# Gathered tokens, gate table and buffers of a PEER layer on Trainium2: 92 instead of 88 tokens gathered, from half of the heads on

## The chip, the cores and the metric

One core of one Trainium2 chip (trn2). The time is that of one execution of the whole program on the device, in microseconds (us). A tile here is 128 x 2048 float32, 1.05 MB.

## The reference

Two blocks on 256 tokens of width 2048, all in float32. Block 1 mixes a short gated convolution with block-sparse attention; block 2 mixes a Conformer convolution with an S5 state-space branch and then adds a PEER layer; a last RMSNorm gives the output. The change lies in the PEER layer: each of 8 heads picks, for each token, 16 of 128 x 128 experts by a product of two key sets, and the experts' rows are combined.

```
q = (xb @ w_q).reshape(PEER_TOKEN_BLOCK, PEER_HEADS, 2, PEER_HALF)
s = jnp.einsum('thcd,hcnd->thcn', q, sub_keys).astype(jnp.float32)
s_top, i_top = lax.top_k(s, PEER_TOPK)
cand = s_top[:, :, 0, :, None] + s_top[:, :, 1, None, :]
...
best, pos = lax.top_k(cand, PEER_TOPK)
expert = jnp.take_along_axis(cand_idx, pos, axis=-1)
gates = jax.nn.softmax(best, axis=-1).astype(xb.dtype)
act = jax.nn.gelu(jnp.einsum('td,thkd->thk', xb, u_tab[expert]))
return jnp.einsum('thk,thkd->td', gates * act, v_tab[expert])
```

## The kernel before

SP streams all weights in an order written out in `order`, one tile a `step()`. The first 192 steps (dense layers, ending with the PEER query projection `peer_q`) split each tile into two parts on ScalarE and VectorE (L189, L195); TensorE then multiplies by `mm_wide` (L293, L294: 512 and 256 columns) or `mm_perm` (L278 to L280: three of 256). Then comes PEER, which treats two sets of tokens in two ways.

**Dense tokens** (168): all 16384 experts are computed. 128 u-steps (L1577) give u.h for 128 experts each, ScalarE applies gelu (L1580), `weigh` (L1391, L1395, VectorE) multiplies by the gate table, and 128 v-steps (L1594) sum into six PSUM banks. The gate table, experts x tokens, is made by `gbuild`: for four tokens at a time, one-hots of their picks (L1348, L1358 on VectorE; L1355 and L1356 on ScalarE), four matmuls that give 128 x 128 tables (L1375), and an evacuation (L1376). Sixteen tokens make a block; eight blocks go to DRAM (`gd`, L1379) and come back per 16 u's (`gload`, L1385); the blocks of the last 40 tokens (`STAY`) remain on chip.

**Gathered tokens** (88, `NS_`): POOL gathers the picked rows of u and v by indirect DMAs (L1416), 128 rows an item, 176 items; for u VectorE takes the dot with the token's h, replicated into `x_rep` (`rows`, L1423; item at L1449), for v it adds the scaled rows (L1461, L1463). Groups of 32, 32, 16 and 8 tokens differ in how many partitions a token has. Five slots take gathers in turn. `hand_out` writes the lists of rows to gather once all eight heads of the first 128 tokens are picked (`topk`, `picks`). At the end `join_rows` adds the partitions of groups 2 and 3 by TensorE (L1516, L1521); those of groups 0 and 1 go to DRAM (`sd`) and back as four quarters (L1488, L1493); then the norm (L1498, L1499) and the output.

The order: 58 u-steps (`NU0`) with top-k and `gbuild` woven in; 70 pairs of one v and one u; 56 v alone; the last two v's go bank by bank in `join` and `turn`, where each bank's sum has the residual (`xq`, loaded at L1628 to L1631) added (L1666), is transposed (L1673) and normed. The class `Weave` interleaves: `gbuild` yields a cost per iteration, and a u-step gives it a budget of 4200; the sparse generator is *paced*: each step credits 0.78 x 2350, an item costs 2350. Each engine runs its instructions in program order, and POOL issues its DMAs in program order. A reference line of a matmul is two instructions on TensorE.

Of the kernel before, what the change touches and what calls it, by code (L numbers as in the profile page):

```python
# [18 lines left out]
P = 128  # L19
# [7 lines left out]
GROUPS = [(0, 32), (32, 32), (64, 16), (80, 8)]  # L27
NS_ = 88
# [16 lines left out]
class Weave:  # L45
# [78 lines left out]
def body(ctx, tc, xT, par, wst, kst, bblk, cblk, gfin, uexp, vexp, out):  # L124
# [104 lines left out]
    free_units = [S[24][:, k * T:(k + 1) * T] for k in range(NRING, 8)]  # L229
# [15 lines left out]
    def step(mm, evac, budget=2600.0, fine=0.0):  # L245
# [8 lines left out]
        ws["n"] += 1  # L254
        pend.append(evac)
# [875 lines left out]
    xrow = drp.tile([NS_, D], F32, name="xrow")  # L1131
    sd = drp.tile([4, 64, D], F32, name="sd")
# [95 lines left out]
    LCOL = [0, 64, 128, 160]  # L1228
    def hand_out(c):


        V = nc.vector
        if c == 0:
            V.scalar_tensor_tensor(out=flat(ab[:, 0]), in0=flat(idx[:, 0]), scalar=float(P), in1=flat(idx[:, 1]),
                                   op0=ALU.mult, op1=ALU.add)
            V.tensor_copy(flat(abu[:, 0]), flat(ab[:, 0]))
        else:
            V.tensor_copy(abr[:, P:2 * P], flat(gat))
        for g in range(2):
            hand_to(c, g)  # L1240
            if c == 0 and g == 0:
                sp_start()
        for g in range(2, len(GROUPS)):
            hand_to(c, g)

    def hand_to(c, g):
# [519 lines left out]
```

## Time and profile before

| | us |
|---|---|
| median of 3 runs (lowest, highest) | 2525.20 (2523.16, 2533.76) |
| profiled execution, its own time | 2530.83 |
| its span on the core | 2528.9 |
| TensorE busy | 2445.0 (97%) |
| VectorE busy | 1586.5 (63%) |
| ScalarE busy | 700.2 (28%) |
| mean granted TensorE clock | 0.991 |

The span is what the profiler saw; the other durations lie within it. Busy time is an average over very different stages; the windows further below tell them apart. A wait is idle time of an engine in front of an instruction, put down to what ended it.

### The profile page before, as it was taken

The numbers are of one execution on the slowest core, as the hardware profiler recorded it, in microseconds if no ns is written. First come the engines' busy times: TensorE is split into PE (matmuls) and PEld (weight loads), VectorE is DVE, ScalarE is ACT, GpSimd is POOL, SyncE is SP. The second block draws the span as 40 slices with busy tenths as digits, with TensorE's granted clock in tenths as the row PEclk, the third lists the DMA queues.
The fourth block names the chain that finished last, engine by engine and source line by source line (L and its number), as shares of the span: only waits on it lengthen the run. The fifth ranks groups of instructions, "written<-read, shape, count | busy, mean of one in ns | idle before, by whom it ended". The sixth has DMA issues, their size and how long they took to land.

```text
span 2528.9 us, 40512 instructions
## 1 busy us (share of the span) xinstructions
PE 2445.0 (97%) x16864; PEld 2322.2 (92%) x16864; DVE 1586.5 (63%) x2764; ACT 700.2 (28%) x1047; POOL 657.0 (26%) x856
## 2 busy tenths in 40 slices
PE   8999999999999999999998999999999999999997
PEld 7888878899999999988998999999999999999887
DVE  6857777589999987657768874534453434324423
ACT  5544455443334445454201640000000000000002
POOL 1788888310000000140122121212122312022000
PEclk9999999999999999999999999999999999999998
DMA  6455555565555444555599999999999999999983
GB/s 237 168 199 184 183 183 210 193 238 210 199 206 179 183 168 181 185 202 193 215 336 418 370 380 417 421 382 421 418 421 415 396 386 414 365 344 398 387 259 125
DMA packets 108187, 719.91 MB, mean 285 GB/s; under 512 B 13308, under 2 KB 14572, under 8 KB 24668
## 3 DMA queue, kind: packets, MB, share of 16 engines
q1 hardware_dynamic: 65764, 474.57, 49.9%
q0 software_dynamic: 34288, 220.73, 22.3%
q10 hardware_dynamic: 7952, 22.02, 2.4%
q8 instruction: 133, 2.18, 0.3%
q14 instruction: 50, 0.41, 0.0%
HBM read 687.10 MB, written 25.91 MB: 282 GB/s over the span
## 4 chain that ended last, share of the span: by engine, by line
PE 71%; DMA 19%; DVE 7%; issue 2%; ACT 1%; POOL 1%; SPq 0%; DVEq 0%; POOLq 0%; ACTq 0%
PE b L1577 14%; PE b L293 13%; PE b L1594 12%; DMA s<-in_vexp_dram 7%; PE b L294 7%; DMA s<-in_wst_dram 6%; PE b L278 4%; PE b L280 4%; PE b L279 4%; DVE s L195 2%; PE b L271 2%; PE b L423 2%; PE b L270 2%; PE b L269 2%; DMA s<-s 2%
## 5 line engine op out<-in xcount | busy, mean ns | idle before, releaser
L1577 PE MATMUL b<-s,s 128*128 128x168 f32 x4096 | 609.2, 308 | 14.0 <-DMA s<-in_wst_dram 13.6
L1594 PE MATMUL b<-s,s 128*128 128x168 f32 x4096 | 605.1, 307 | 17.3 <-DMA s<-in_vexp_dram 15.9
L1594 PEld LDWEIGHTS b<-s,s 128*128 128x128 f32 x4096 | 588.3, 190 | 30.4 <-issue 27.0
L1577 PEld LDWEIGHTS b<-s,s 128*128 128x128 f32 x4096 | 590.6, 191 | 21.4 <-issue 20.4
L293 PE MATMUL b<-s,s 128*128 128x512 f32 x1680 | 599.7, 400 | 0.0
L294 PE MATMUL b<-s,s 128*128 128x256 f32 x1680 | 472.0, 281 | 9.6 <-DVE s L195 9.6
L195 DVE TENSOR_TENSOR s<-s,s 128x2048 fp32r<-128x2048 f32 x192 | 453.3, 2363 | 27.2 <-issue 12.5
L293 PEld LDWEIGHTS b<-s,s 128*128 128x128 f32 x1680 | 316.1, 188 | 72.8
L189 ACT ACTIVATE s<-s 128x2048 fp32r<-128x2048 f32 x192 | 365.7, 1905 | 9.6 <-DMA s<-in_wst_dram 9.1
L1449 DVE CUSTOM_DVE_ANT_0 s<-s,s 128x2048 f32<-128x2048 f32 x88 | 201.1, 2290 | 261.0 <-DMA s<-in_uexp_dram,rbuf 209.9
L294 PEld LDWEIGHTS b<-s,s 128*128 128x128 f32 x1680 | 317.7, 189 | 13.8 <-DVE s L195 13.0
L1463 DVE SCALAR_TENSOR_TENSOR s<-s,sqsum,s 128x2048 f32<-128x2048 f32 x84 | 197.4, 2350 | 120.8 <-DMA s<-in_vexp_dram,rbuf 120.3
L1580 ACT ACTIVATE s<-b 128x168 f32<-128x168 f32 x128 | 39.1, 307 | 803.7 <-PE b L1577 803.7
L278 PE MATMUL b<-s,s 128*128 128x256 f32 x896 | 256.6, 286 | 0.0
L280 PE MATMUL b<-s,s 128*128 128x256 f32 x896 | 253.5, 283 | 0.0
L279 PE MATMUL b<-s,s 128*128 128x256 f32 x896 | 253.5, 283 | 0.0
L1416 POOL DMA_INDIRECT s<-in_uexp_dram,rbuf x88 | 110.5, 1256 | 394.6 <-DVE s L1463 218.0
L1416 POOL DMA_INDIRECT s<-in_vexp_dram,rbuf x88 | 103.1, 1171 | 316.5 <-DVE sqsum L1449 224.6
L278 PEld LDWEIGHTS b<-s,s 128*128 128x128 f32 x896 | 171.8, 192 | 3.7 <-issue 2.9
L279 PEld LDWEIGHTS b<-s,s 128*128 128x128 f32 x896 | 171.9, 192 | 0.3
L280 PEld LDWEIGHTS b<-s,s 128*128 128x128 f32 x896 | 171.9, 192 | 0.0
L837 POOL TENSOR_TENSOR sqsum<-sqsum,s 128x256 f32<-128x256 f32 x28 | 59.4, 2120 | 389.7 <-ACT s L835 389.7
(310 smaller groups left out, 2511.8 us busy)
## 6 DMA issues: line engine op xcount, KB each, us to landing
s<-in_wst_dram SPq DMA_DIRECT2D x320, 1024.0 KB, 5.0
s<-in_vexp_dram SPq DMA_DIRECT2D x128, 1024.0 KB, 17.4
tabd<-s POOLq DMA_DIRECT2D x32, 256.0 KB, 4.5
s<-tabd ACTq DMA_DIRECT2D x32, 256.0 KB, 3.5
gd<-s ACTq DMA_DIRECT2D x8, 1024.0 KB, 9.9
s<-gd POOLq DMA_DIRECT2D x7, 1024.0 KB, 27.0
xd<-s POOLq DMA_DIRECT2D x4, 1024.0 KB, 9.8
s<-in_bblk_dram ACTq DMA_DIRECT2D x8, 512.0 KB, 3.6
```

The lines of the kernel that those rows point to most:

```text
L189: nc.scalar.activation(hi_of(i), raw_of(i), AF.Copy)
L195: nc.vector.tensor_tensor(out=lo_of(i), in0=raw_of(i), in1=FV(hi_of(i)), op=ALU.subtract)
L278: nc.tensor.matmul(ps, a, xh, start=(j == 0), stop=False)
L279: nc.tensor.matmul(ps, a, xl, start=False, stop=False)
L280: nc.tensor.matmul(ps, b, xh, start=False, stop=(j == len(perm) - 1))
L293: nc.tensor.matmul(ps, a, x2, start=(j == 0), stop=False)
L294: nc.tensor.matmul(ps[:, :T], b, x2[:, :T], start=False, stop=(j == len(perm) - 1))
L1416: nc.gpsimd.indirect_dma_start(out=gb[m % len(gb)][:], out_offset=None, in_=uexp if kind == "u" else vexp, in_offset=bass.IndirectOffsetOn ...
L1449: V.tensor_tensor_reduce(out=buf, in0=buf, in1=x_rep, scale=1.0, scalar=0.0, op0=ALU.mult, op1=ALU.add, accum_out=dots_[:, k:k + 1])
L1463: V.scalar_tensor_tensor(out=acc_s, in0=buf, scalar=a, in1=acc_s, op0=ALU.mult, op1=ALU.add)
L1577: nc.tensor.matmul(ps, raw[:, k * P:(k + 1) * P], nv(k)[:, NS_:T], start=(k == 0), stop=(k == KT - 1))
L1594: nc.tensor.matmul(acc[d], raw[:, d * P:(d + 1) * P], act_at(i), start=False, stop=(i == P - 1 and (d % 3 == 2 or d == KT - 1)))
```

## The change

- **Tokens**: a fifth group of 4 tokens; `NS_` 92, 184 items, 164 dense tokens. Its h rows go to 32 x 4 partitions by 32 DMAs. At a group's boundary the last v items come before the first u items of the next group, but for the last group. All h rows now come from a copy in DRAM (`hrow`).
- **Gathers**: they may start after four heads (`number`, `told`); the item loop waits in program order for what isn't told yet. Buffers come from a free list: four at first, two more after the scores, four again during `gbuild`, five after. Weight slots have a free list, too. Pace 0.74.
- **Gate table**: six blocks through DRAM, laid out so that a load serves 8 u's in one run; 68 tokens stay on chip in five pieces. Two one-hots of four on ScalarE; yield 1350 for 1650.
- **`peer_q`**: tiles 2 to 15 by `mm_perm`.
- **End**: `xrow` is loaded into another slot once 84 v's are issued, the sums of group 2 are joined later, the quarters are added at 800 a piece.

The order of u- and v-steps is the same as before. Renamed slots are left out below.

```diff
-GROUPS = [(0, 32), (32, 32), (64, 16), (80, 8)]
-NS_ = 88
+GROUPS = [(0, 32), (32, 32), (64, 16), (80, 8), (88, 4)]
+NS_ = 92
...
-        self.pace, self.paced_credit = 0.78 * 2350, 0
+        self.pace, self.paced_credit = 0.74 * 2350, 0
...
-    NSP = 8
-    STAY = [16, 16, 8]
+    NSP = 6
+    STAY = [16, 16, 16, 16, 4]
...
-    gd = drp.tile([NSP, P, P, 16], F32, name="gd")
+    gd = drp.tile([16, P, NSP, 8, 16], F32, name="gd")
...
+        nc.gpsimd.dma_start(hrow, S[18][0:NS_, :])
+        rows(0)
...
+    def number(h):
+        hs = slice(h, h + 4)
+        nc.vector.scalar_tensor_tensor(out=ab[:, 0, hs], in0=idx[:, 0, hs], scalar=float(P), in1=idx[:, 1, hs],
+                                       op0=ALU.mult, op1=ALU.add)
+        nc.vector.tensor_copy(by_part(ids, hs), parts4(ab[:, 0, hs]))
...
-                if h == 5:
+                if h == 4:
                     yield from picks(tt, 0)
+                    if tt == 0:
+                        number(0)
+                        hand_to(0, 0, 0, 16)
+                        told.add("first")
             yield from picks(tt, 4)
             if tt == 0:
-                hand_out(0)
+                number(4)
+                hand_to(0, 0, 16, 32)
+                for g in range(1, len(GROUPS)):
+                    hand_to(0, g)
+                told.add("all")
...
     def gbuild():
+        retired.update([13, 18])
+        free_b[:] = [b for b in free_b if b not in retired]
...
-                if q < 1:
+                if q < 2:
                     nc.scalar.activation(o, iota, AF.Abs, scale=-1.0, bias=i1T[:, tq])
                     nc.scalar.activation(o, o, AF.Relu, scale=ngT[:, tq], bias=gT[:, tq])
...
-            yield 1650
+            yield 1350
...
-        if i % 16 == 15 and i // 16 + 2 < 8:
-            gload(i // 16 + 2, nc.gpsimd)
+        if i % 8 == 7 and i // 8 + 2 < 16:
+            gload(i // 8 + 2, nc.gpsimd)
...
-        for kind, m in (("u", j), ("v", j - 1)):
+        pair = [("u", j), ("v", j - 1)]
+        if 0 < j < len(batches) - 1 and batches[j][0] != batches[j - 1][0]:
+            pair.reverse()
+        for kind, m in pair:
...
+    def gathers():
+        while free_b and n_gathered[0] < len(items):
+            kind, g, k = items[n_gathered[0]]
+            if "all" not in told and not ("first" in told and g == 0 and k < 16):
+                return
+            b = free_b.pop(0)
+            nc.gpsimd.indirect_dma_start(
...
             nc.gpsimd.dma_start(x_rep[n * q:n * q + n, :], S[18][t0:t0 + n, :])
+            nc.gpsimd.dma_start(x_rep[n * q:n * q + n, :], hrow[t0:t0 + n, :])
...
-        gb.extend(slots([5, 6, 7, 12, 13]))
+        free_b.extend([6, 5, 7, 18])
...
+            while n_gathered[0] <= m or (kind == "v" and "gates" not in told):
+                gathers()
+                yield None
...
-                    sums.append((m + 3, g))
+                    sums.append((m + (6 if g == 2 else 3), g, acc_s))
...
+                while n_v[0] <= 7 * TPS:
+                    yield None
...
-            yield 2350
+            yield 800
...
-        ps = mmbank2(1)
-        step(lambda wh, wl: mm_wide(ps, wh, wl, pv2, allk), ev_pq(ps, j), TOP)
+        ps = mmbank()
+        step(lambda wh, wl: mm_perm(ps, wh, wl, pv, allk), ev_pq(ps, j), TOP)
+    sp_start()
```

How the order of instructions moves, at three places. In these listings `s_...` are slots, `b_...` PSUM banks.

ScalarE in `gbuild`, between two u-steps' gelus; before (L1376 evacuates, L1355 and L1356 make a one-hot, L1580 is the gelu):

```order
L1376 ACTIVATE s_10081<-b_71 128x4x128
L1355 ACTIVATE s_10080<-iota,s_86 128x128
L1356 ACTIVATE s_10080<-s_10080,s_86 128x128
L1580 ACTIVATE s_10973<-b_66 128x168
L1376 ACTIVATE s_10081<-b_72 128x4x128
L1355 ACTIVATE s_10080<-iota,s_86 128x128
L1356 ACTIVATE s_10080<-s_10080,s_86 128x128
L1376 ACTIVATE s_10081<-b_71 128x4x128
```

The same now (L1406, L1385 and L1386, L1642):

```order
L1406 ACTIVATE s_10074<-b_72 128x4x128
L1385 ACTIVATE s_10081<-iota,s_87 128x128
L1386 ACTIVATE s_10081<-s_10081,s_87 128x128
L1385 ACTIVATE s_10081<-iota,s_87 128x128
L1386 ACTIVATE s_10081<-s_10081,s_87 128x128
L1642 ACTIVATE s_11208<-b_65 128x164
L1406 ACTIVATE s_10074<-b_71 128x4x128
```

Two one-hots, each of two operations, stand between two evacuations where one stood.

POOL, the h rows of the last group in front of its gathers; before, sixteen DMAs of 8 rows for group 3 (L1423; L1416 gathers, L1385 loads the gate table):

```order
L1416 DMA s_11192<-in_vexp_dram,rbuf 128x2048
L1416 DMA s_11193<-in_uexp_dram,rbuf 128x2048
L1423 DMA s_10077<-s_10076 8x2048 x16
L1385 DMA s_10073<-gd 128x8x256
L1416 DMA s_11194<-in_uexp_dram,rbuf 128x2048
L1416 DMA s_11195<-in_uexp_dram,rbuf 128x2048
L1416 DMA s_11196<-in_uexp_dram,rbuf 128x2048
```

Now, thirty-two of 4 rows for group 4 (L1464; L1455 gathers, L1415 loads the gate table):

```order
L1455 DMA s_11197<-in_vexp_dram,rbuf 128x2048
L1455 DMA s_11198<-in_uexp_dram,rbuf 128x2048
L1464 DMA s_10078<-hrow 4x2048 x32
L1455 DMA s_11196<-in_uexp_dram,rbuf 128x2048
L1455 DMA s_13153<-in_uexp_dram,rbuf 128x2048
L1415 DMA s_10074<-gd 128x768
L1455 DMA s_11360<-in_uexp_dram,rbuf 128x2048
L1455 DMA s_11197<-in_vexp_dram,rbuf 128x2048
```

Three of the four u gathers of the last group and all eight v gathers behind them (of which two are shown) wait on POOL behind the copies.

VectorE at the end of the sparse tokens; before, the last add of a join (L1521), then the quarters (L1493) with weighs (L1391, L1395) of later v's between and behind them:

```order
L1521 TENSOR_TENSOR s_16426<-s_16426,b_65 24x512
L1521 TENSOR_TENSOR s_16426<-s_16426,b_66 24x512
L1493 TENSOR_TENSOR s_16426<-s_16426,s_11192 64x2048
L1391 TENSOR_TENSOR s_10971<-s_10971,s_12891 128x128
L1395 TENSOR_TENSOR s_10971<-s_10971,s_11862 128x16
L1395 TENSOR_TENSOR s_10971<-s_10971,s_10081 128x16
L1395 TENSOR_TENSOR s_10971<-s_10971,s_86 128x8
L1391 TENSOR_TENSOR s_10971<-s_10971,s_12891 128x128
```

Now (L1512 the last item, L1579 the join of group 4, L1550 the quarters, L1556 the norm's product):

```order
L1512 SCALAR_TENSOR_TENSOR s_17696<-s_11196,sqsum,s_17696 128x2048
L1579 TENSOR_TENSOR s_16844<-s_16844,b_65 28x512
L1579 TENSOR_TENSOR s_16844<-s_16844,b_66 28x512
L1579 TENSOR_TENSOR s_16844<-s_16844,b_65 28x512
L1579 TENSOR_TENSOR s_16844<-s_16844,b_66 28x512
L1550 TENSOR_TENSOR s_16844<-s_16844,s_11197 64x2048
L1550 TENSOR_TENSOR s_16844<-s_16844,s_11196 64x2048
L1550 TENSOR_TENSOR s_16844<-s_16844,s_11198 64x2048
L1550 TENSOR_TENSOR s_16844<-s_16844,s_11360 64x2048
L1556 TENSOR_TENSOR s_16844<-s_16844,s_17455 92x2048
```

All weighs stand in front of this piece, as do the first joins' adds; only the norm stands between it and the closing's first add (now L1729). On TensorE the joins' matmuls stand behind the 126th v-step.

## Rows read from the trace of the kernel before

**Rows 1.** Windows by stage: start, length, busy per engine (instructions), PEclk, DMA share, GB/s.

```profile
1229.00:1545.60 316.60, 308.11 (x2215) 307.16 (x2214) 235.15 (x600) 99.88 (x207) 67.10 (x71) 0.98 0.91 352
1400.00:1470.00 70.00, 70.00 (x539) 70.00 (x538) 55.72 (x117) 48.25 (x90) 9.28 (x8) 1.00 0.98 373
1545.60:2220.10 674.50, 653.94 (x4480) 640.69 (x4480) 287.12 (x474) 22.72 (x83) 153.45 (x136) 1.00 1.00 403
2220.10:2499.10 279.00, 268.60 (x1811) 259.86 (x1810) 97.47 (x253) 6.62 (x10) 39.78 (x51) 0.99 0.92 330
...
2499.10:2528.90 29.80, 14.12 (x98) 12.22 (x96) 12.87 (x34) 9.12 (x28) 0.00 (x0) 0.78 0.13 47
```

**Rows 2.** TensorE's waits, 1545 to 2529 us: total us, times, longest.

```profile
PE b L1594 <- DMA s<-in_vexp_dram: 15.9, 34, 2.4
PE b L1577 <- DMA s<-in_wst_dram: 13.6, 28, 3.9
```

**Rows 3.** VectorE's waits, 1545 to 2529 us, same columns.

```profile
DVE s L1449 <- DMA s<-in_uexp_dram,rbuf: 196.6, 56, 44.6
...
DVE s L1463 <- DMA s<-in_vexp_dram,rbuf: 110.3, 45, 12.3
```

**Rows 4.** Timeline of TensorE, gate table and v stage: start, us, line, shapes, count.

```profile
1405.29 2.45 PE L1577 MATMUL b<-s,s 128*128 128x168 f32 x16
1407.57 1.05 PE L1375 MATMUL b<-s 128*128 128x128 f32 x8
1408.46 1.31 PE L1577 MATMUL b<-s,s 128*128 128x168 f32 x8
...
2299.56 4.83 PE L1594 MATMUL b<-s,s 128*128 128x168 f32 x32 [0.20 <-DVE s L1395]
2304.54 7.66 PE L1594 MATMUL b<-s,s 128*128 128x168 f32 x49 [0.15 <-DVE s L1395]
```

**Rows 5.** Timeline of ScalarE in the gate table: evacuation, then a one-hot.

```profile
1441.04 1.06 ACT L1376 ACTIVATE s<-b 128x512 f32<-128x512 f32 x1 [0.98 <-PE b L1375]
1441.89 0.37 ACT L1355 ACTIVATE s<-iota,s 128x128 f32<-128x128 f32 x1
1442.30 0.49 ACT L1356 ACTIVATE s<-s,s 128x128 f32<-128x128 f32 x1
```

**Rows 6.** Timeline of TensorE, triples at 799 us, pairs at 1047 us.

```profile
799.08 0.28 PE L278 MATMUL b<-s,s 128*128 128x256 f32 x1
...
802.67 0.28 PE L278 MATMUL b<-s,s 128*128 128x256 f32 x1
...
1047.68 0.40 PE L293 MATMUL b<-s,s 128*128 128x512 f32 x1
...
1053.68 0.40 PE L293 MATMUL b<-s,s 128*128 128x512 f32 x1
```

**Rows 7.** Timeline of POOL: first list, loads of xq, rows of group 3.

```profile
1252.60 2.02 POOL L1254 DMA_DIRECT2D rbuf<-s  x4 [114.70 <-DVE s L1310]
...
2218.30 0.94 POOL L1628 DMA_DIRECT2D s<-xd  x1 [45.73 <-PE b L1577]
...
2263.08 0.52 POOL L1423 DMA_DIRECT2D s<-s  x1 [6.25 <-DMA s<-in_uexp_dram,rbuf]
...
2271.27 0.52 POOL L1423 DMA_DIRECT2D s<-s  x1 [1.17 <-DMA s<-s]
```

**Rows 8.** Timeline of VectorE, group 3's first item and the end.

```profile
2284.68 2.29 DVE L1449 CUSTOM_DVE_ANT_0 s<-s,s 128x2048 f32<-128x2048 f32 x1 [25.30 <-DMA s<-s]
...
2451.11 0.69 DVE L1521 TENSOR_TENSOR s<-s,b 24x512 f32<-24x512 f32 x1 [44.47 <-PE b L1516]
...
2452.89 0.33 DVE L1395 TENSOR_TENSOR s<-s,s 128x16 f32<-128x16 f32 x3
...
2458.96 2.28 DVE L1493 TENSOR_TENSOR s<-s,s 64x2048 f32<-64x2048 f32 x1
...
2500.99 0.68 DVE L1666 TENSOR_TENSOR s<-b,s 128x504 f32<-128x504 f32 x1 [24.39 <-PE b L1594]
```

More of the change, by code (lines that the diff above doesn't have):

```diff
@@ L228, in body @@
     NRING = 4
-    free_units = [S[24][:, k * T:(k + 1) * T] for k in range(NRING, 8)]
+    free_units = [S[25][:, k * T:(k + 1) * T] for k in range(4)]
     free_pairs = []
@@ L254, in step @@
         ws["n"] += 1
+        if i in whole:
+            w_release(i)
         pend.append(evac)
@@ L1227, in body, with hand_to @@
     flat = lambda ap: ap.rearrange("p h k -> p (h k)")
[L1228 to L1246, printed above, removed]
+    LCOL = [0, 64, 128, 160, 176]
+    ids = mask.bitcast(U32)
+    by_part = lambda ap, hs: ap.rearrange("p (q h j) -> p h q j", q=4, h=8)[:, hs]
+    parts4 = lambda ap: ap.rearrange("p h (q j) -> p h q j", q=4)
+    def number(h):
[3 more added lines that the diff above has]
+        nc.vector.tensor_copy(by_part(ids, hs), parts4(ab[:, 0, hs]))
+    def hand_to(c, g, k0=0, k1=None):
         t0, n = GROUPS[g]
@@ L1316, in topk @@
             if tt == 0:
-                hand_out(1)
+                V.tensor_copy(by_part(abr[:, P:2 * P], slice(0, 8)), parts4(gat))
+                for g in range(len(GROUPS)):
+                    hand_to(1, g)
+                told.add("gates")
             yield None
@@ L1347, in gbuild @@
             t = NS_ + t4 * 4
+            if t4 == 4 * (NSP + 2):
+                while retired & set(flying):
+                    next(sp_gen)
+                kept[2:4] = slots([18, 13])
             nc.vector.tensor_tensor(
@@ L1422, in rows @@
         for q in range(P // n):
-            nc.gpsimd.dma_start(x_rep[n * q:n * q + n, :], S[18][t0:t0 + n, :])
+            nc.gpsimd.dma_start(x_rep[n * q:n * q + n, :], hrow[t0:t0 + n, :])
     def sp_start():
-        assert ws["n"] >= WU and len(q_ready) == KT and s_ready[0] == NH
-        gb.extend(slots([5, 6, 7, 12, 13]))
-        for m in range(len(gb)):
-            gather(m)
-            if m == 0:
-                rows(0)
+        assert ws["n"] == WU
+        slots([6, 5, 7, 18, 3, 4])
+        free_b.extend([6, 5, 7, 18])
+        w_free.extend([3, 4])
+        gathers()
         weave.paced.append(sp_gen)
@@ L1435, in sparse @@
         V = nc.vector
+        more = [12, 13]
         for _ in range(AHEAD):
+            gathers()
             yield None
@@ L1466, in sparse @@
                 nc.scalar.activation(dst, src, AF.Gelu_apprx_tanh)
-            if m + len(gb) < len(items):
-                gather(m + len(gb))
+            if b not in retired:
+                free_b.append(b)
+            if more and s_ready[0] == NH:
+                slots(more)
+                free_b.extend(more)
+                more = []
+            gathers()
             if kind == "u" and k == n - 1 and g < len(GROUPS) - 1:
@@ L1481, in sparse @@
                 yield 2350
-                yield from join_rows(sums.pop(0)[1], acc_s)
+                yield from join_rows(*sums.pop(0)[1:])
             yield 2350
         y = y_rows[0]
+        gb = [S[b] for b in (5, 6, 7, 12)]
         quarters = [gb[q][0:64, :] for q in range(4)]
@@ L1490, in sparse @@
             yield None
-        yield from join_rows(sums.pop(0)[1], acc_s)
+        yield from join_rows(*sums.pop(0)[1:])
         for q in range(4):
             V.tensor_tensor(out=y[0:64, :], in0=y[0:64, :], in1=quarters[q], op=ALU.add)
-            yield 2350
+            yield 800
         while not gf_there[0]:
@@ L1511, in join_rows @@
         t0, n = GROUPS[g]
-        assert u_done[0]
-        s_ = sel[:, 96 * (g - 2):96 * (g - 2) + NS_]
+        while not u_done[0]:
+            yield None
+        s_ = sel[:, NS_ * (g - 2):NS_ * (g - 1)]
         for h in range(2):
@@ L1651, in body @@
     ws["n"] += LAST
-    zs = slots([15, 16])
-    rows_o = slots([17, 8])
+    zs = slots([9, 23])
+    rows_o = slots([10, 17])
     junk = slots([12])[0]
```

123 lines of the change are left out of this document (70 added, 53 removed).

## The prediction

> **What bounds the kernel now.** I first read the windows by stage, then TensorE's waits, VectorE's waits, and last the timelines of the stages that the change touches. The stages [rows 1] are: 58 u-steps with top-k and gate table (316.6 us), 70 pairs of v and u (674.5), 56 v-steps alone (279.0), and the closing (29.8). TensorE is busy for 308.11 of 316.6, 653.94 of 674.5 and 268.60 of 279.0 us, at a granted clock of 0.98 to 1.00, its level of 2.4 GHz: its own work is the first bound. In the pairs the DMA engines are the second, with a share of 1.00 and 403 GB/s. TensorE's waits there and after are small: 15.9 and 13.6 us for weight tiles [rows 2]. VectorE in the same time waits 196.6 and 110.3 us for gathered rows [rows 3]. So both the SP queue (weights) and the POOL queue (gathers) are always filled, and a tile of 1.05 MB costs 2.60 us of DMA time (1.0486 MB / 403 GB/s). When TensorE does wait for weights, it steps at 4.98 us (2299.56 to 2304.54) instead of its own 4.56, twice the 2.28 us of 16 instructions [rows 4].
>
> **Fewer columns.** A u- or v-step is 32 instructions of 168 columns, now 164. 16 instructions of 168 columns take 2.28 us and 8 of 128 columns 0.89 us [rows 4], 142.5 and 111.2 ns each, so 0.78 ns per column; 32 x 4 x 0.78 = 0.10 us a step, and 4.46 in place of 4.56. Over 256 steps that is 25.6 us, wherever TensorE is the bound.
>
> **Query projection** (`mm_wide` to `mm_perm`). A pair of instructions takes 0.353 us (17 in 6.00 us), a triple 0.359 (10 in 3.59) [rows 6]. For 16 triples in each of 14 tiles that is +1.3 us; I take +1. The ACT copy and the VectorE add that it drops lie beside TensorE and cost nothing now.
>
> **U stage with the gate table.** By the first pair of order fences ScalarE now makes two of four one-hots: four short operations and one evacuation per four tokens instead of two and one. From start to start an evacuation takes 0.85 us, the next operation 0.41, the last at most 0.49 [rows 5]. So an iteration costs 0.85 + 2 x (0.81 to 0.90) = 2.47 to 2.65 us, plus one gelu of the u-step per 3.1 iterations (0.1 us): 2.56 to 2.74. TensorE needs 0.89 + 4.46/3.11 = 2.32 us per iteration, because the smaller yield packs 3.11 iterations into a u-step where 2.55 were (counted in the order). So ScalarE, at 48.25 of 70 us busy before [rows 1], becomes the bound of this stretch. I take the middle, 2.65: 41 x 2.65 = 109 us for the stretch, and (58 - 41/3.11) x 4.46 = 200 us for the other u-steps. Before: 42 x (0.89 + 4.56/2.55) = 113 and (58 - 42/2.55) x 4.56 = 189. Together 309 against 302: **+7**. The ends: -7 (295) if ScalarE keeps up, +10 (312) at 2.74. VectorE loses a one-hot per iteration, which hid beside TensorE. Earlier gathers (first at 1252.60 before [rows 7], after the last of the eight heads) use idle DMA time, but the order has 40 items on VectorE ahead of the first weigh (37 before) and 143 of 184 ahead of the 72nd, where the u's end (145 of 176): the slower pace of 0.74 gives the lead back.
>
> **Pairs.** By TensorE 140 x 0.10 = -14 us. By DMA 103 items instead of 108 between those two places, 5 x 2.60 = -13. Both bounds fall alike, so I take **-13**; the other end is 0, if each saved column is waited out on weights that still come at 4.98.
>
> **V stage and closing.** Here two paths run. The sparse path now: at 2220 VectorE had 31 items left, now 41. It ended with time to spare: 44.47 us of waiting for TensorE before a join, and 24.39 before the closing's first operation at 2500.99 [rows 8]. Without the first of these the closing could have begun 281 - 44 - 24 = about 212 us after 2220. Added are 10 gathers at 5.0 us, the queue's turn while both queues are full (50 us), one more join (4.3, estimated: four adds of 0.69 us [rows 8] and the matmuls that the second pair of them waits for), and the h rows of the fifth group: 32 small DMAs on POOL, in front of the gathers (second pair of fences). Group 3's sixteen are the nearest rows. Once they run, POOL issues one per 1.02 us (nine from 2263.08 to 2271.27 [rows 7]) and VectorE idled 25.30 us for them [rows 8], 1.58 each. So 33 to 51 us, with 32 x 0.52 = 17 as the floor if only the issue counts. I take 42, because the copies are half as large but as many waits stand between them. What is queued behind: gathers 173 and on, and on VectorE the weighs of the last v-steps, for which TensorE then waits too. Against it: the loads of `xq`, for which POOL waited 45.73 us on TensorE's last u-step [rows 7], block less when the sparse path is late; I take 15 of a possible 31. So 212 + 50 + 4 + 42 - 15 = 293.
> The Trainium skill, "DMA: Bandwidth & Descriptors", section "Anatomy of one DMA — SWDGE (gpsimd) path", gives a DMA issued from GpSimd about 2.0 us plus its bytes at 436 GB/s, so 32 in a row would take 66 us and the sum would be 24 us higher; the issues at 1.02 us show that several overlap here, so I do not take it.
> TensorE's path: 54 x 4.46 = 241 us and 5 to 21 of waits. But two joins and the token sums now stand behind the 126th v-step (third pair): 4.3 for a join, 2.3 for the last item, 4.3 again, 4 x 2.28 for the sums [rows 8] and some 5.5 for the norm (two operations of that length and 1 us) make 25.5 us before the closing's first add. Before, this lay in the 24 and 44 us of slack, at no cost. So 272 to 288. The later of the two paths counts: 293 against 281, and the closing behind it is the same: **+12**, with ends -9 (272, all gathers in time) and +36 (51 us of copies and no relief from `xq`, 317).
>
> **Cost nothing:** the gate blocks now come in 16 loads of 0.39 MB for 7 of 1 MB, with fewer bytes; two more weigh operations a step (three took 0.33 us [rows 8], so 0.22) on a VectorE that waits for gathers; `hrow` to DRAM, 0.75 MB beside the projection. If their cover, VectorE's 300 us of waiting, were gone, the weighs would cost 128 x 0.22 = 28 us.
>
> **Sum:** 1 + 7 - 13 + 12 = +7 on the profiled execution's 2530.8, so 2537.8. That execution lies 5.6 above the median of 2525.2; I give the median, **2532 us**.
>
> **Rivals.**
> *Faster* (0.31): ScalarE does not bind and the sparse path is done in time. For: VectorE's 44 us of slack [rows 8], and the short activations [rows 5] may follow each other faster than they did with idle time between. Against: ScalarE's sum above 2.32, and the joins behind the last steps. With the middle of 272 to 288 for the end, 1 - 7 - 14 - 1 = -21: 2504 us.
> *Slower* (0.27): the 32 row copies. Three gathers of u and eight of v stand behind them, and the last weighs, and TensorE behind those. For: 25.30 us of idle for sixteen. Against: they leave the DMA engines to the weights, so TensorE gains a lead. At 51 us with no relief: 1 + 7 - 13 + 36 = +31: 2556. It decides from about 45 us on, where the sparse path passes 300 us.
> *It doesn't do what it says* (0.06): during the gate table only four gather buffers are in turn. If the gathers are bound by their flight, four instead of five give a quarter longer per item: about 22 items x 1.1 us = 24 us, 2557. For: VectorE's waits for gathers [rows 3]. Against: in the U stage VectorE was busy 235.15 of 316.6 [rows 1] and the pace sets items.
> *My forecast*, no change that can be told: 0.36.
>
> **Range and chances.** A measurement of this kernel tells about 0.5% from no change, 12.6 us. The range of 2502 to 2560 takes in the middle of the faster case and the whole of the slower ones but the worst sums of ends; about a tenth is left out on each side. The forecast alone, with its ends for ScalarE (-14 and +3) and for the xq loads (-16 and +15), would give 2516 to 2547. Faster 0.31; same 0.36; slower 0.33, the two slow cases together.
>
> **What would show it.** Right: u-steps of 4.46 us; in the gate-table stretch TensorE waits for ScalarE's one-hots, and an iteration takes 2.5 to 2.7 us; pairs 13 us shorter; VectorE idle for the last row copies 30 to 50 us; the closing's first add 25 us or more behind the 126th v-step. Wrong: iterations of 2.32 us with no wait on ScalarE; row copies inside 20 us; the closing right behind the last v-step; or pairs as long as before, with waits for weights that ate the columns.

## The result, and the profile after

The changed kernel takes 2544.0 us (median of 7 runs, 2539.26 to 2556.5) against 2525.4 before (7 runs): a ratio of 1.0076, 95% interval 1.0054 to 1.0097. It is 19 us slower. Its profiled span is 2541.0 us against 2528.9, so 12 of the 19 us are in the traces compared here.

The stages in the profile after, in windows cut at the same places as [rows 1] (first u-step, first v-step, last u-step, end of the 126th v-step, end); the second row is a piece of the gate table's stretch. Columns are as there.

```profile
1230.40:1550.20 319.80, 306.52 (x2206) 301.33 (x2205) 223.83 (x542) 126.06 (x287) 68.80 (x73) 0.99 0.90 345
1400.00:1470.00 70.00, 65.91 (x485) 62.63 (x484) 45.94 (x92) 66.15 (x145) 5.76 (x5) 1.00 0.84 278
1550.20:2209.10 658.90, 635.31 (x4482) 624.46 (x4481) 286.80 (x621) 22.35 (x81) 173.05 (x136) 1.00 1.00 403
2209.10:2478.30 269.20, 257.65 (x1803) 251.28 (x1802) 105.85 (x339) 3.99 (x9) 64.78 (x91) 1.00 0.99 374
2478.30:2541.00 62.70, 27.24 (x112) 17.53 (x110) 35.87 (x62) 14.50 (x33) 2.71 (x5) 0.71 0.27 71
```

Against [rows 1]: the u stage 3.2 us longer, the pairs 15.6 shorter, the v stage 9.8 shorter, and the closing 62.7 in place of 29.8, 32.9 longer. With the 1.4 us of the projection that is +12.1, the difference of the spans. The change won 25 us in two stages and lost 33 behind the last full v-step. The 1.4 us of the projection and the 3.2 of the u stage are no more than other runs of the same code, below, differ by.

The piece of VectorE's timeline that answers to [rows 8], in the profile after (L1496 an item of u, L1512 an item of v, L1579 a join, L1550 the quarters, L1729 the closing's first add):

```profile
2423.03 2.29 DVE L1496 CUSTOM_DVE_ANT_0 s<-s,s 128x2048 f32<-128x2048 f32 x1 [35.99 <-DMA s<-hrow]
...
2481.20 2.35 DVE L1512 SCALAR_TENSOR_TENSOR s<-s,sqsum,s 128x2048 f32<-128x2048 f32 x1 [2.20 <-DMA s<-in_vexp_dram,rbuf]
2483.58 1.29 DVE L1579 TENSOR_TENSOR s<-s,b 28x512 f32<-28x512 f32 x2
...
2488.53 2.35 DVE L1512 SCALAR_TENSOR_TENSOR s<-s,sqsum,s 128x2048 f32<-128x2048 f32 x1
...
2497.05 9.24 DVE L1550 TENSOR_TENSOR s<-s,s 64x2048 f32<-64x2048 f32 x4
...
2511.93 0.67 DVE L1729 TENSOR_TENSOR s<-b,s 128x492 f32<-128x492 f32 x1
```

VectorE stands idle for 35.99 us until the fifth group's h rows are there, where group 3 cost 25.30. Then the last items, two joins, the sums and the norm follow one another until 2511.93, 33.6 us behind the 126th v-step (2478.3); before it was 1.9. The two waits of [rows 8] that were slack, 44.47 and 24.39 us, are gone. POOL shows the loads of `xq` (L1689), the copies (L1464), then the first gather behind them:

```profile
2207.37 0.96 POOL L1689 DMA_DIRECT2D s<-xd  x1 [42.98 <-PE b L1639]
...
2375.73 3.65 POOL L1464 DMA_DIRECT2D s<-hrow  x6
...
2411.09 1.15 POOL L1464 DMA_DIRECT2D s<-hrow  x2 [0.58 <-DMA s<-hrow]
2414.48 1.00 POOL L1455 DMA_INDIRECT s<-in_uexp_dram,rbuf  x1 [2.23 <-DMA s<-hrow]
```

From the first copy to the item that needs them it is 47.3 us (2375.73 to 2423.03). In the kernel before it was 46.5 us for group 3's sixteen copies, up to 2284.68 in [rows 8], though VectorE was idle for only 25.30 of them:

```profile
2238.14 1.61 POOL L1423 DMA_DIRECT2D s<-s  x3
```

TensorE's waits from 1229 us to the end, total, times and longest:

```profile
PE b L1656 <- DMA s<-in_vexp_dram: 19.9, 32, 3.4
PE b L1736 <- DVE s L1729: 16.8, 4, 13.0
PE b L1639 <- DMA s<-in_wst_dram: 12.1, 25, 2.5
PE b L1345 <- DVE s L1336: 7.2, 1, 7.2
PE b L1405 <- ACT s L1386: 5.9, 21, 0.7
```

The last row is new: in the gate table TensorE now waits for ScalarE's one-hots. The waits for weight tiles (19.9 and 12.1 us) did not fall with the columns. TensorE's matmuls of the v stage alone, and two steps of the pairs in its timeline:

```profile
L1656 PE MATMUL b<-s,s 128*128 128x164 f32 x1792 | 254.5, 303 | 11.6 <-DMA s<-in_vexp_dram 8.6 <-DVE s L1425 2.9
```

```profile
2195.77 4.62 PE L1639 MATMUL b<-s,s 128*128 128x164 f32 x32
2200.23 4.62 PE L1656 MATMUL b<-s,s 128*128 128x164 f32 x32
```

At 32 instructions a step, 1792 are 56 v-steps. From start to start a step takes 4.46 us.

### The profile page after: what moved, and what is told of

Same layout as the page of the kernel before. It is cut to its first block, busy times and chain, and to the rows that moved or that the text cites. A ratio compares the mean times of both kernels' runs of the same rounds, so it can differ in the third digit from the quotient of the medians.

```text
span 2541.0 us, 41363 instructions
## 1 busy us (share of the span) xinstructions
PE 2429.0 (96%) x17088; PEld 2309.2 (91%) x17088; DVE 1607.2 (63%) x2981; ACT 729.5 (29%) x1129; POOL 710.1 (28%) x912
## 4 chain that ended last, share of the span: by engine, by line
PE 68%; DMA 18%; DVE 8%; ACT 5%; issue 1%; POOL 0%; ACTq 0%; SPq 0%; DVEq 0%; POOLq 0%
PE b L1656 12%; PE b L301 12%; PE b L1639 11%; DMA s<-in_vexp_dram 7%; PE b L302 6%; PE b L286 5%; PE b L288 5%; PE b L287 5%; DMA s<-in_wst_dram 5%; DMA s<-in_vexp_dram,rbuf 3%; PE b L279 2%; PE b L431 2%; PE b L278 2%; PE b L277 2%; DVE s L201 2%
## 5 line engine op out<-in xcount | busy, mean ns | idle before, releaser
L1656 PE MATMUL b<-s,s 128*128 128x164 f32 x4096 | 591.0, 304 | 23.0 <-DMA s<-in_vexp_dram 19.9
L1639 PE MATMUL b<-s,s 128*128 128x164 f32 x4096 | 592.8, 304 | 12.1 <-DMA s<-in_wst_dram 12.1
L301 PE MATMUL b<-s,s 128*128 128x512 f32 x1456 | 521.1, 401 | 0.0
L302 PE MATMUL b<-s,s 128*128 128x256 f32 x1456 | 409.9, 282 | 9.6 <-DVE s L201 9.6
L1496 DVE CUSTOM_DVE_ANT_0 s<-s,s 128x2048 f32<-128x2048 f32 x92 | 210.2, 2288 | 235.1 <-DMA s<-in_uexp_dram,rbuf 199.1
L286 PE MATMUL b<-s,s 128*128 128x256 f32 x1120 | 320.7, 286 | 0.0
L288 PE MATMUL b<-s,s 128*128 128x256 f32 x1120 | 317.0, 283 | 0.0
L287 PE MATMUL b<-s,s 128*128 128x256 f32 x1120 | 316.9, 283 | 0.0
L302 PEld LDWEIGHTS b<-s,s 128*128 128x128 f32 x1456 | 276.2, 190 | 13.4 <-DVE s L201 12.8
L1512 DVE SCALAR_TENSOR_TENSOR s<-s,sqsum,s 128x2048 f32<-128x2048 f32 x87 | 204.3, 2348 | 112.8 <-DMA s<-in_vexp_dram,rbuf 112.0
L1642 ACT ACTIVATE s<-b 128x164 f32<-128x164 f32 x128 | 39.0, 305 | 806.6 <-PE b L1639 806.5
L1455 POOL DMA_INDIRECT s<-in_uexp_dram,rbuf x92 | 124.9, 1357 | 459.2 <-DVE s L1512 246.5
L1455 POOL DMA_INDIRECT s<-in_vexp_dram,rbuf x92 | 118.6, 1289 | 320.2 <-DVE sqsum L1496 240.0
## 6 DMA issues: line engine op xcount, KB each, us to landing
s<-in_vexp_dram SPq DMA_DIRECT2D x128, 1024.0 KB, 16.3
s<-gd POOLq DMA_DIRECT2D x14, 384.0 KB, 23.5
```

The lines of the kernel that those rows point to most:

```text
L286: nc.tensor.matmul(ps, a, xh, start=(j == 0), stop=False)
L287: nc.tensor.matmul(ps, a, xl, start=False, stop=False)
L288: nc.tensor.matmul(ps, b, xh, start=False, stop=(j == len(perm) - 1))
L301: nc.tensor.matmul(ps, a, x2, start=(j == 0), stop=False)
L302: nc.tensor.matmul(ps[:, :T], b, x2[:, :T], start=False, stop=(j == len(perm) - 1))
L1455: nc.gpsimd.indirect_dma_start(out=S[b][:], out_offset=None, in_=uexp if kind == "u" else vexp, in_offset=bass.IndirectOffsetOnAxis(ap=gad ...
```

## The experiments

All are edits of the changed kernel; each was timed in 4 to 12 runs, beside the kernel before on the same chip. Their medians are set against 2544.0 us. They come from four chips, on which the median of the kernel before was 2525.1 to 2527.4 us, so a difference of 2 or 3 us between two medians says little; the ratio to the kernel before is given beside each. The stage lengths come from their profiles, in the windows used above, and a profiled execution can lie 7 us off its kernel's median. The u stage of the same code varies by some 6 us between profiles (319.8 in the changed kernel, 323.6 to 325.9 in four runs below that keep it), with the one wait for top-k (L1345) between 7 and 16 us, and the first u-step comes at 1225.6 to 1230.4 us; smaller differences there mean nothing.

**e1: the fifth group's rows by 4 DMAs.**

```diff
+        if g == 4:
+            for c in range(4):
+                nc.gpsimd.dma_start(x_rep[32 * c:32 * c + 32, :],
+                                    hrow[None, t0:t0 + n, :].to_broadcast([8, n, D]))
+            return
```

> The h rows of the fifth group come by 4 DMAs of 32 partitions (the 4 rows repeated by a stride of zero) in place of 32 DMAs of 4 rows; all else as in the changed kernel. Theory A (two paths end one after the other: the row copies, then the joins and sums that the order puts behind the 126th v-step): the 36.0 us for which VectorE idled on the copies fall to under 10, the sparse path is then early, and the closing's first add comes about 25 us behind the 126th v-step instead of 33.6: 4 to 12 us faster than the changed kernel, still slower than or level with the kernel before. Theory B (the copies are all of the loss; the order of the joins costs nothing by itself): the closing follows the 126th v-step within 5 us, 20 us or more faster. Theory C (the gathers bound the end whatever the copies do): no change within 3 us.

2540.6 us (ratio to the kernel before 1.0057, 1.0038 to 1.0075), 3.4 under the changed kernel: between theory A's 4 and theory C's 3, and not clear of the noise. Its v stage, and VectorE's timeline of this run (L1501 the item of u, L1584 the join, L1734 the closing's first add):

```profile
2211.40:2483.50 272.10, 260.39 (x1801) 254.40 (x1800) 108.99 (x346) 3.99 (x9) 54.32 (x64) 0.99 0.98 372
```

```profile
2403.95 2.29 DVE L1501 CUSTOM_DVE_ANT_0 s<-s,s 128x2048 f32<-128x2048 f32 x1 [11.58 <-DMA s<-hrow]
...
2484.38 0.69 DVE L1584 TENSOR_TENSOR s<-s,b 28x512 f32<-28x512 f32 x1 [20.04 <-PE b L1579]
...
2512.50 0.67 DVE L1734 TENSOR_TENSOR s<-b,s 128x492 f32<-128x492 f32 x1
```

The idle time for the copies falls from 36 to 11.58 us, and the sparse items are early: VectorE waits 20.04 us for the join's matmuls, which stand behind the 126th v-step (end at 2483.5). From there to the closing it is 29.0 us, 4.6 less than 33.6. So theory A holds for the closing: behind the copies stands a second path, TensorE's, with the joins that the order puts last. Counted from the last u-step the closing's first add comes at 301.1 us (272.1 + 29.0), in the changed kernel at 302.8: the two paths end within 2 us of each other.

**e2: one of four one-hots on ScalarE, as before.**

```diff
-                if q < 2:
+                if q < 1:
```

> One of four one-hots on ScalarE, as before the change, with everything else (the yield of 1350 too) as changed. Theory A (ScalarE bounds the gate-table stretch at 2.61 us per four tokens): the iteration falls to TensorE's 2.32 us, 41 x 0.29 = 12 us in the stretch, and the time by 8 to 12 us if nothing behind takes it back. Theory B (VectorE, with three one-hots more per iteration than it can fit beside the gathered items, becomes the bound): no gain in the stretch, same time within 3 us. Theory C (the stretch gains, but the gathers, which set the end, don't come sooner): the stretch 10 us shorter and the time 0 to 5 us lower.

2536.3 us (1.0048, 1.0035 to 1.0062), 7.7 under the changed kernel. The stretch from the first to the last matmul of the gate table takes 92.7 us in place of 104.7. The same 70 us of it in this run, and the whole stretch:

```profile
1383.00:1476.00 93.00, 93.00 (x733) 92.78 (x732) 78.11 (x172) 71.30 (x133) 8.08 (x7) 1.00 0.91 316
1400.00:1470.00 70.00, 70.00 (x550) 69.79 (x549) 60.21 (x131) 54.23 (x102) 6.08 (x6) 1.00 0.94 325
```

TensorE is busy for 70.00 of 70 us (65.91 in the changed kernel) and does 550 instructions where it did 485; ScalarE falls from 66.15 to 54.23. VectorE takes the third one-hot without becoming the bound. The 7.7 us lie just under theory A's 8 to 12 and above theory C's 0 to 5. In the profile the whole u stage is only 2.8 us shorter (317.0), because the wait for top-k was 16.3 us in this one and 7.2 in the changed kernel's; against the four profiles of 323.6 to 325.9 it is 7 to 9.

**e3: no early start of the gathers.**

```diff
-                        told.add("first")
```

> The gathers start only when all eight heads are picked, as before the change; free lists, pace and all else as changed. Theory A (the early start's lead is given back by the slower pace, and only the items' places count): 140 items in place of 143 stand ahead of the 72nd weigh, three gathers more for the end at 5.0 us: 5 to 15 us slower than the changed kernel. Theory B (the gathers are far enough ahead in the u stage that a later start is caught up): same within 3 us. If the early start did harm by taking POOL and DMA time from the top-k stage: faster.

2574.2 us (1.0197, 1.0177 to 1.0218): 30 us slower than the changed kernel, twice what theory A allowed and against B. Nearly all of it is in the u stage, 345.5 us in place of 319.8:

```profile
1229.40:1574.90 345.50, 312.96 (x2207) 307.41 (x2205) 219.61 (x540) 125.63 (x286) 68.38 (x71) 0.95 0.82 311
```

The DMA engines' share there is 0.82 for 0.90, and the granted clock 0.95 for 0.99. VectorE waits 28.5 us there for gathered rows of u, where it waited 10.5. This is not the arrangement of the kernel before, where `sp_start` puts the whole loop of items later: here the items keep nearly all their places, so VectorE waits in front of them. How this reaches TensorE the trace shows (L1514 is the gelu of gathered items on ScalarE, L1641 that of a u-step, L1638 the u-step):

```profile
1303.40 0.20 ACT L1514 ACTIVATE sqsum<-sqsum 128x4 f32<-128x4 f32 x1 [14.28 <-DVE sqsum L1495]
...
1343.16 0.20 ACT L1514 ACTIVATE sqsum<-sqsum 128x4 f32<-128x4 f32 x1 [18.47 <-DVE sqsum L1495]
```

```profile
1343.62 34.44 PE L1638 MATMUL b<-s,s 128*128 128x164 f32 x224 [10.36 <-ACT s L1641]
```

ScalarE waits for the dots of late items, the gelus of u-steps stand behind that wait in its order, and TensorE waits for them, 16.6 us in two waits that the changed kernel does not have. The rest of the 26 us is a longer wait for top-k (10.2 us for 7.2) and 6.4 us more of TensorE's own work (312.96 for 306.52) at the lower clock.

**e4: 88 tokens, no fifth group; all else as changed.**

```diff
-GROUPS = [(0, 32), (32, 32), (64, 16), (80, 8), (88, 4)]
-NS_ = 92
+GROUPS = [(0, 32), (32, 32), (64, 16), (80, 8)]
+NS_ = 88
...
-    STAY = [16, 16, 16, 16, 4]
+    STAY = [16, 16, 16, 16, 8]
```

> 88 gathered tokens without the fifth group, all other parts of the change kept (68 tokens become 72 on chip, 168 dense tokens). Theory A (the fifth group costs 33 us at the end by its copies and its place behind the 126th v-step, and gives back 0.10 us in each step that TensorE bounds): in the order the joins stand behind the 121st and 122nd v-step, so the closing follows the last v-step as before the change, 30 us saved there, against about 4 + 0 to 14 + 5 us of columns: 10 to 22 us faster than the changed kernel, about level with the kernel before. Theory B (the columns are worth their full 25.6 us): 5 us faster or less. Theory C (the DMA engines bound everything from the u stage on): the eight gathers left out save 40 us.

2520.4 us (0.9974, 0.9962 to 0.9986): 23.6 under the changed kernel, a little beyond theory A's 22, and 0.26% under the kernel before. Its stages:

```profile
1229.50:1550.70 321.20, 312.52 (x2215) 307.47 (x2214) 224.71 (x544) 129.12 (x292) 64.95 (x69) 0.99 0.89 344
1550.70:2210.60 659.90, 648.72 (x4484) 639.12 (x4483) 286.93 (x621) 22.53 (x81) 177.76 (x136) 1.00 0.99 402
2210.60:2490.80 280.20, 269.11 (x1809) 262.62 (x1809) 108.77 (x349) 5.67 (x11) 41.74 (x55) 0.98 0.92 333
2490.80:2520.40 29.60, 13.76 (x97) 12.06 (x95) 12.87 (x34) 10.15 (x29) 0.56 (x1) 0.83 0.20 71
```

The closing is 29.6 us again. And the pairs take 659.9 us with 168 columns where the changed kernel takes 658.9 with 164: TensorE is busy 13.4 us less there (635.31 against 648.72), and all but 1 us of it became waiting. TensorE's waits in the pairs, in e4 and then in the changed kernel:

```profile
PE b L1656 <- DMA s<-in_vexp_dram: 5.5, 15, 1.6
PE b L1639 <- DMA s<-in_wst_dram: 4.1, 15, 1.8
```

```profile
PE b L1639 <- DMA s<-in_wst_dram: 12.1, 25, 2.5
PE b L1656 <- DMA s<-in_vexp_dram: 11.4, 20, 3.4
```

They are waits for weight tiles, 9.6 us and 23.5. **The columns are worth nothing in the pairs.** The 15.6 us that the pairs gained on the kernel before fit the slower pace, with fewer gathers in them: at 403 GB/s both times, 15.6 us are 6.3 MB, six tiles. e12 tests the pace by itself.

**e5 and e6: the last items earlier in the order.** From the last u-step on, the pace is 1.0; e6 has the 4 copies of e1, too.

```diff
                 u_done[0] = True
+                weave.pace = 1.0 * 2350
```

> Only the place of the last sparse items in the program order is changed: from the last u-step on the pace is 1.0 item a step in place of 0.74, so the joins stand behind the 113th and the 121st v-step in place of the 126th; the 32 row copies stay. Theory A (after the first runs: the loss is the chain of joins, sums and norm that the order puts between the 126th v-step and the closing, some 25 us, and the copies are a smaller second): the closing's first add follows the 126th v-step within 12 us in place of 33.6; some of it comes back as TensorE's waits for weighs that stand behind the copies: 12 to 28 us faster than the changed kernel. Theory B (the gathers end too late wherever their items stand in the order, so that only the waits move from the closing to the v-steps): the same within 5 us.

> The pace of e5 and the 4 row copies of e1 together. Theory A: both losses of the end are gone, 25 to 35 us faster than the changed kernel, the closing as close behind the 126th v-step as in the kernel before (1.9 us), so 5 to 15 us under the kernel before. Theory B (gathers too late): at most 8 us faster than the changed kernel, with TensorE waiting 10 us or more for weighs in the v stage.

e5: 2554.5 us (1.0126, 1.0107 to 1.0145), slower than the changed kernel by 10. e6: 2543.3 (1.0081, 1.0066 to 1.0097), the same. The v stage and closing of e5, then of e6:

```profile
2211.30:2521.10 309.80, 270.52 (x1818) 262.03 (x1817) 129.91 (x378) 6.92 (x12) 67.01 (x96) 0.94 0.94 334
2521.10:2550.60 29.50, 13.74 (x96) 11.84 (x95) 12.79 (x34) 9.12 (x28) 0.00 (x0) 0.79 0.14 51
```

```profile
2210.50:2507.30 296.80, 270.50 (x1818) 260.06 (x1818) 130.19 (x378) 6.92 (x12) 56.95 (x68) 0.96 0.95 349
2507.30:2537.20 29.90, 14.44 (x97) 12.25 (x95) 12.79 (x34) 9.11 (x28) 0.00 (x0) 0.75 0.14 50
```

The closing is hidden again, 29.5 and 29.9 us, exactly as wanted. But the v stage grew by what was won: 309.8 and 296.8 us where e1 had 272.1 (and 56.9 for the closing). TensorE's longest wait in e5's v stage:

```profile
PE b L1656 <- DVE s L1425: 34.1, 5, 16.3
```

It now waits for weighs, which stand behind items that wait for gathers. e6 fits theory B in both its numbers (0.7 us faster, 13.6 us of waits for weighs). e5 is slower than either theory allowed, but the mechanism is theory B's: the order only chooses where the wait falls. The granted clock fell too, to 0.94 in e5, and the v-steps' matmuls took longer:

```profile
L1656 PE MATMUL b<-s,s 128*128 128x164 f32 x1794 | 260.7, 309 | 35.5 <-DVE s L1425 34.1 <-DMA s<-in_vexp_dram 1.4
```

Moving the joins was not the mend I took it for after e1.

**e7 and e8: the mends together.** e7 is e6 with one of four one-hots on ScalarE and 4 row copies for the groups of 16 and 8 tokens too; e8 is e4 with the same two edits, and no change of pace.

> As e6, with one of four one-hots on ScalarE (e2) and with 4 row copies for the groups of 16 and 8 tokens too. Theory A: the gains add: a further 6 to 12 us for the gate table and 0 to 4 for the rows, 2500 to 2512 us in all. Theory C (what the gate table gains is taken back by gathers that are not sooner): as e6 within 3 us.

> 88 tokens as in e4, with one of four one-hots on ScalarE and 4 row copies for the groups of 16 and 8 tokens. The end is hidden here already, so the gate table's 12 us should show nearly whole: 8 to 13 us under e4's 2520.4. If 92 tokens pay at all, e7 is 3 us or more under this run: 256 x 0.10 = 25.6 us of columns against what the weights' share of the DMA engines takes back.

e7: 2524.7 us (0.9998, 0.9986 to 1.0011), 18.6 under e6. That is more than the gains that theory A added up, but its 2500 to 2512 in all was missed, because e6 stood higher than forecast. By stage the u stage is 11.8 us shorter than e6's and the v stage 7.7. e8: **2509.3** (0.9944, 0.9929 to 0.9960), 11 under e4, as forecast. So 92 tokens don't pay: with the same mends, and the pace of 1.0 that hides their joins, they are 15 us behind 88. Nearly all of it lies in the v stage, e7's and then e8's:

```profile
2200.30:2489.40 289.10, 269.62 (x1818) 260.60 (x1818) 130.11 (x378) 6.92 (x12) 56.07 (x56) 0.95 0.96 358
```

```profile
2197.40:2473.10 275.70, 268.51 (x1811) 261.58 (x1810) 108.54 (x349) 5.76 (x11) 39.16 (x43) 0.99 0.91 339
```

**e9 to e11: the loads of `xq` 28 v-steps before the end of the v's**, 30 v-steps later than before. POOL waits 43.0 us for the last u-step with these loads in the changed kernel, and the gathers queue behind. e9 is e6 with this edit; e10 adds e7's edits with a pace of 0.9 in the v stage; e11 is e8 with it.

```diff
-                xq = slots([20, 21])
-                nc.gpsimd.dma_start(xq[0][:, 0:8 * NT].rearrange("p (d t) -> p d t", d=8),
...
             continue
+        if i == P - 28:
+            xq = slots([20, 21])
+            nc.gpsimd.dma_start(xq[0][:, 0:8 * NT].rearrange("p (d t) -> p d t", d=8),
```

> e6 (pace 1.0 from the last u-step on, 4 row copies) with one more edit: the loads of the residual xq are issued on POOL 30 v-steps later, so that no gather stands behind a DMA that waits for TensorE's last u-step (43.0 us of POOL's time in e6, the gather queue empty for some 30). Theory D (the v stage is bound by the supply of gathers: 41 items left at its start, five buffers, and this hole in front of them; that is why e5 and e6 only moved the wait from the closing to the weighs): the v stage falls from 296.8 us by 20 to 30, the closing stays hidden, 18 to 30 us under e6. Theory E (the DMA engines' bytes bound the v stage, hole or not): at most 6 us under e6.

> 92 tokens with all mends: xq loads 30 v-steps later, 4 row copies for the groups of 16, 8 and 4 tokens, one of four one-hots on ScalarE, pace 0.9 in the v stage. Theory D: e7's 2524.7 less 18 to 28 us, so 2497 to 2507, level with or under the best run of 88 tokens before it (2509). Theory E: 2520 to 2527.

> e8 (88 tokens, 4 row copies, one of four one-hots on ScalarE) with the xq loads 30 v-steps later. Its sparse path had 80 us of slack at its joins, so theory D expects little: 0 to 8 us under e8's 2509.3, from a stage start without weighs that wait. If the hole is worth 20 us here too, it delayed weighs, not only the end of the sparse path.

e9: 2527.4 us (0.9997, 0.9983 to 1.0010), 15.9 under e6 by the medians and 21 by the ratios (1.0081 and 0.9997), about the low end of theory D's 18 to 30. Its v stage, and TensorE's waits for weighs in e6 and then in e9:

```profile
2211.70:2493.90 282.20, 268.45 (x1818) 257.46 (x1819) 121.06 (x354) 6.81 (x12) 53.85 (x58) 0.99 0.96 358
```

```profile
PE b L1661 <- DVE s L1425: 13.6, 6, 9.2
```

```profile
PE b L1661 <- DVE s L1425: 1.8, 1, 1.8
```

The v stage falls from 296.8 us to 282.2 with the closing still hidden, so the hole in the gather queue was a cause of the waits. e10: 2522.7 (0.9981, 0.9969 to 0.9994), only 2 under e7, where theory D asked for 18 at least; E's number fits. But e10 also has a pace of 0.9 where e7 has 1.0: its v stage is 9 us shorter than e7's (279.9) and its closing 11 longer (40.3), so what the later loads are worth beside the other mends is not shown by it. e11: 2509.5 (0.9927, 0.9905 to 0.9949), as e8: with 88 tokens they are worth nothing that can be told.

**e12: the pace of 0.78 back, in e10.**

> e10 with the pace before the v stage put back from 0.74 to 0.78 items a step: 150 items in place of 143 stand ahead of the 72nd weigh. Theory F (the v stage lacks DMA time, 41 gathers and 56 weight tiles in 241 us of TensorE's work, while the u stage has some idle: 302 GB/s in the gate table's stretch against 403 in the pairs): the items that move forward into the u stage are gained, 3 x 5.0 = 15 us, those that move into the pairs cost there what they save later: 6 to 16 us under e10's 2522.7. Theory G (from the start of the pairs on the DMA engines are full, and the u stage can't take more with four gather buffers): the pairs 10 us longer, the v stage 10 us shorter, the time within 4 us of e10.

2526.2 us (0.9997, 0.9980 to 1.0014). The stages of e10, then of e12:

```profile
1543.80:2206.20 662.40, 639.87 (x4482) 627.66 (x4480) 295.26 (x639) 22.35 (x81) 182.60 (x143) 0.99 1.01 407
2206.20:2486.10 279.90, 265.47 (x1818) 254.13 (x1819) 111.94 (x339) 2.60 (x8) 47.51 (x45) 1.00 0.95 354
2486.10:2526.40 40.30, 16.68 (x97) 14.44 (x95) 21.40 (x44) 13.21 (x32) 0.56 (x1) 0.72 0.15 52
```

```profile
1556.70:2231.50 674.80, 644.85 (x4483) 628.45 (x4482) 299.52 (x624) 22.45 (x82) 183.10 (x143) 0.99 1.01 405
2231.50:2501.30 269.80, 263.83 (x1819) 255.30 (x1818) 110.81 (x361) 4.50 (x9) 41.98 (x41) 0.99 0.92 350
2501.30:2531.70 30.40, 13.75 (x97) 11.80 (x95) 15.11 (x41) 11.21 (x30) 0.56 (x1) 0.84 0.20 69
```

The pairs are 12.4 us longer, v stage and closing 20 shorter in this profile, whose u stage is 13.8 longer, about twice what profiles of one code differ by; the medians differ by 3.5 us, within theory G's 4, and theory F's gain is not there. The pairs of 674.8 us are those of the kernel before to 0.3 us, at its pace, though with 164 columns for its 168: again the pace sets them, not the columns. The pace alone is worth 12.4 of the 15.6 us by which the changed kernel's pairs were shorter.

Not tested alone are the query projection, the free lists, the layout of the gate blocks and the order of items at a group's boundary.

## Why the prediction came out as it did

The forecast was 2532 us, no change that can be told, in a range of 2502 to 2560; the kernel takes 2544.0, 0.76% slower, which had a chance of 0.33. The direction of the sum (+7) was right, the size was not (+12 in the profile, +19 in the medians). Of the 12 us by which the median misses the forecast, 5 are in the traces (2542.8 against 2537.8 us); the other 7 come from profiled executions, which lay 5.4 us above the median before and 1.3 below it after. By its steps:

- **Fewer columns**: the step is 4.46 us where nothing waits, as predicted (against e4, TensorE has 13.4 us less work in the pairs, where 14 were forecast). That this would be time won failed: e4 and e12 show none of it in the pairs.
- **Query projection**: +1 predicted; the first u-step comes 1.4 us later, which is inside the spread of 1225.6 to 1230.4 in other profiles of the same projection. Neither shown nor refuted.
- **U stage with the gate table**: +7 predicted, +3.2 in this profile, which is the shortest of five, and +7 to +9 in the four runs that repeat the same code (323.6 to 325.9, against the one profile of before). ScalarE binds, as the sum said: e2 wins 12.0 us in the stretch, and 41 iterations in 104.7 us are 2.55 us each, the low end of 2.56 to 2.74. The other sentence, that the slower pace gives the early start's lead back, is not decided: e3 shows that the early start is worth 30 us once the items have these places, and no run has the early start with the places of the kernel before.
- **Pairs**: -13 predicted, -15.6 measured. But of the two bounds that "fall alike" only the DMA one holds. With equal prices the trace of before could not tell them apart; e4 does.
- **V stage and closing**: +12 predicted, +23.1 measured (269.2 + 62.7 against 279.0 + 29.8). This is the step that was mis-sized. The two paths are the right picture, but both were forecast too short, and the closing's first add came 302.8 us behind the last u-step, against 293 forecast and 281 before.
  - *The sparse path*: the relief from `xq` was hardly there. I had taken 15 us; POOL waited 42.98 us against 45.73. The copies were no dearer than forecast: VectorE was idle 36.0 us for them, and I had taken 42. Without relief and with 36 the sum is 212 + 50 + 4 + 36 = 302.
  - *TensorE's path*: the sum has 54 v-steps behind the last u-step, and there are 56, so 250 us and not 241. The joins and the norm were sized at 25.5 us; e1 shows 29.0 with the copies out of the way. Redone with 56 steps the path ends at 280 to 296 us, where e1 shows 301.1.
  - So the forecast was short by 9 us through a count and by 15 through a relief of which the run had 3 at most, and each path alone ends at 301 to 303 us. The 212 and the 50 of the sparse path are not measured apart.
- **Price of the copies**: the trace shows 47.3 us from the first issue to the item for 32 copies, 1.5 each, and 36.0 us of it as idle time of VectorE, 1.1 each. Group 3's row, 1.02 to 1.58 each, was a good price. The Trainium skill, "DMA: Bandwidth & Descriptors", section "Anatomy of one DMA — SWDGE (gpsimd) path", gives a DMA issued from GpSimd about 2.0 us plus its bytes at 436 GB/s, which makes, as an estimate, 66 us for 32 one after the other. The trace does not agree with that for copies issued in a row.

What the forecast did not weigh is where the trade is paid. From the pairs on the DMA engines are full (share 1.00 in the pairs, 0.99 in the changed v stage), and with 92 tokens eight more items are left for the v stage (35 from 2200 us on in the changed kernel, 27 in e4), while the columns that pay for them are TensorE's time, which is not short in the pairs. With the same mends 92 tokens stay 15 us behind 88 (e7 against e8), 13 of them in the v stage; that the eight items are the cause there fits their number, but no run changes them alone. The slower rival, the 32 copies, named the place and not the cause: with 4 copies the closing's first add still comes at 301.1 us and the time falls by 3.4 (e1). That the order of the joins would be a loss by itself was not so either: moved forward beside late gathers, they gained nothing (e5, e6).

The whole intervals of e4, e8, e10 and e11 lie under the kernel before. The fastest are e8 and, the same within the noise, e11. e8 has 88 tokens, the early start, free lists and gate table of the change, one of four one-hots on ScalarE, and row copies by a repeating source. It takes 2509.3 us, 0.56% under the kernel before (0.40 to 0.71).

## What to carry to other kernels

When a change moves work from one engine to a queue, price it where both are full: 13 us less of TensorE's work in the pairs came out as 12 us more of waiting, while a slower pace of gathers, which looked like a side effect, was the gain there. Count the steps of each path from the program before multiplying, and give a term of relief a row of its own or leave it out. A chain that is hidden at the end has a length and a place in the order; look at what it costs when the items in front of it come 20 us later, and test the place and the supply apart, because moving one without the other only moves the wait. Many small DMAs that replicate one thing can be a few with a repeating source: here 4 for 32, and 11.6 us of idle time for 36.0.

## What the runs showed of the hardware

- A copy of 4 rows to 128 partitions by 32 DMAs from DRAM kept VectorE idle for 36.0 us, by 4 DMAs of the same bytes for 11.6; from first issue to the item it was 47.3 us against 22.9 (2381.05 to 2403.95 in e1).
- A dependent pair of activations on 128 x 128 starts about every 0.80 us when ScalarE has no idle time (1402.39 to 1403.19 in the changed kernel), the low end of the price taken from the trace of before; the evacuation of 128 x 512 takes 0.83 from start to start (1404.01 to 1404.84).
- In a stage with long waits of TensorE the granted clock is lower: 0.94 on the mean of e5's v stage, with 34.1 us of waits for weighs (the longest 16.3 us), so part of it ran at 1.2 GHz; it was 1.00, all at 2.4 GHz, in the changed kernel's, with 11.6 us of waits of at most 2.3 us. Nearly the same number of v-step matmuls took 260.7 us for 254.5, so the waits cost about 6 us beyond their own length. The rest of the 40.6 us by which e5's v stage is longer is 28 us more of waiting and the two more joins in it.
- In the pairs a tile of 1.05 MB costs 2.60 us of the DMA engines at a share of 1.00 (403 GB/s, before and after), so 13.4 us less of TensorE's work gave 1 us.
